# Hybrid attention block: 16 differences of x on VectorE instead of GpSimd, and another order of the weight sums in the token units

## The chip, the cores and the metric

The kernel runs on one core of a Trainium2 chip. The metric is the device time of one execution in microseconds (us). A core has five engines with a queue of instructions each: TensorE (PE in the profile: matmuls; PEld is its loading of weights), VectorE (DVE), ScalarE (ACT), GpSimd (POOL) and SyncE (SP), which here issues nearly all DMAs. Each queue is worked off in order; an instruction waits for the semaphores of what it needs, and everything behind it on its engine waits with it.

## The reference

One decoder block on x of 1024 tokens by 1024 channels, in float32. All projections of the first half come from the same normalised input:

```python
xn = rmsnorm(x, norm1_g[l])
qa, ka, va, qr, kr, vr, gr, gate_a, gate_b = [xn @ wl[:, bounds[i]:bounds[i + 1]] for i in range(len(IN_SPLITS))]
...
y = jax.nn.sigmoid(gate_a) * (o_a @ w_proj_a[l]) + jax.nn.sigmoid(gate_b) * (o_r @ w_proj_b[l])
x = x + y @ w_out[l]
xn2 = rmsnorm(x, norm2_g[l])
x = x + jnp.square(jax.nn.relu(xn2 @ w_up[l])) @ w_down[l]
```

`qa`, `ka`, `va` are the 12 heads of the dilated attention, the others belong to the retention and the gates. The change touches only how `xn`, and the weights of `qa`, `ka` and `va`, are made ready for the products.

## The kernel before

**Products in three matmuls.** Each float32 operand is split in a high part (ScalarE, L365, `xh` or `wh`) and a low part (VectorE, L368, `xl` or `wl`), and each product is three matmuls: high by high, high by low, low by high (L268). A split thus needs ScalarE first and then VectorE.

**Seven products for eight.** Most projections use a Strassen-Winograd scheme: a product of 2 by 2 blocks takes seven block products, N1 to N7, on sums and differences of the blocks. The operands N1, N2 and N3 are blocks of x as they are; N5, N7, N6 and N4 are made of differences and sums. The same holds on the side of the weights, where a token unit has the blocks x11, x12, x21, x22, y12 and y22 (names of the code; "x" there is a weight block, too).

**The values' stage** (start to about 74 us). The eight tiles of 128 tokens are taken in the order 0, 4, 1, 5, 2, 6, 3, 7; steps below are numbered 0 to 7 in this order, and so are the tiles. For each tile: load, sum of squares on ScalarE (L610), scale and offset on VectorE (L381), power -1/2 on GpSimd (L382, 128x1), norm on VectorE in two halves (L613, `xn`), transposes on PE (L545, `tr`) in two groups q = 0 and 1, split of the transposes (L365, L368), and a copy `x` of them (L554). Meanwhile PE runs one step for each tile: 24 matmuls that give the first four heads' values, copied out by VectorE (L638, `c`). Behind every second tile, `differences` makes the four operands N5, N7, N6 and N4 of that pair: on GpSimd one subtraction or addition of 128x512 each (L566), then a split of the result.

**The token units** (behind it). Four units `u` of 1024 columns (queries and keys of head pairs, and the other heads' values). Each runs N1, N2, N6, N5, N3, N7, N4, and for each name four groups `t` of 12 matmuls. Their results go in turn to two pools of PSUM banks, `mm` and `ms`, three banks each; VectorE adds them up (L716 for N2, L719 to L732 for the rest). A result that belongs to queries or keys is squared by ScalarE into another bank of `ms` (L690), reduced by VectorE (L691), scaled by GpSimd (L382, L694), and four groups later transposed by PE (L661).

**The weights** are handled by the class `Weights`. `add_tokens` writes down, for each unit, in which order blocks are loaded and in which place of SBUF (0 to 5; a place is free for the next load when its block is in `used`), and a list of steps: each step does the sums of its operand (L121) and its split, into one of six pairs of buffers. A pair is free when PE is through with the unit in it. `p` is 0 or 1: each block has two halves of 512 rows.

**What sets the order.** PE's queue is as written in the program. On the other engines a scheduler puts the instructions in order when the program is built, by its own costs; `keep_in_program_order` pins an instruction, so that it isn't moved ahead or behind others that way. A pinned split pins its ScalarE part.

Of the kernel before, what the change touches and what calls it, by code (L numbers as in the profile page):

```python
# [13 lines left out]
OP = mybir.AluOpType  # L14
# [23 lines left out]
class Weights:  # L38
# [58 lines left out]
    def add_tokens(self, tag, srcs):  # L97

        for u, quads in enumerate(srcs):
            r = {}  # L100
            second = [("x21", 0, 4), ("x22", 0, 2), ("x21", 1, 5), ("x22", 1, 3)]
            if u == 0:
                second = [second[i] for i in (0, 2, 1, 3)]
            for name, p, place in (("x11", 0, 0), ("x11", 1, 1), ("x12", 0, 2), ("x12", 1, 3), *second,
                                   ("y12", 0, 2), ("y12", 1, 3), ("y22", 0, 2), ("y22", 1, 3)):
                r[name, p] = len(self.src)
                self.src.append(quads[{"11": 0, "12": 1, "21": 2, "22": 3}[name[1:]]][p])
                self.place.append(place)
            for name, x, need, ends, sums in (
# [4 lines left out]
                for p in range(2):  # L114
                    buf, key = self.cycle[self.turn % self.WB], (tag, u, name, p)
                    self.turn += 1

                    def step(p=p, x=x, ends=ends, sums=sums, buf=buf, key=key, r=r):
                        for y, z in sums:
                            y, z = self.raw[r[y, p]], self.raw[r[z, p]]  # L120
                            self.nc.vector.tensor_tensor(y, y, z, op=OP.add)  # L121
                        h, l = self.buffer(buf)
                        self.split(h, l, self.raw[r[x, p]])
                        self.units[key] = h, l
                        self.used.update(r[e, p] for e in ends)

                    self.steps.append((self.claim(buf, key), r[need, p], step))
# [124 lines left out]
class Pipe:  # L252
# [24 lines left out]
    def step(self, ps, terms, ends=None, first=True):  # L277
        fns = self.due.pop(self.slot, [])
        n, m = len(terms), len(fns)
        place = {}  # L280
        for j, fn in enumerate(fns):
            place.setdefault(min(n - 1, (j + 1) * n // (m + 1)), []).append(fn)

        def after(i):
            for fn in place.get(i, []):
                fn()
            if ends and i in ends:
                ends[i]()

        self.group(ps, terms, after, first)  # L290
        self.slot += 1
# [23 lines left out]
def hybrid_block(ctx: ExitStack, tc: tile.TileContext, a: dict, out: bass.AP):  # L315
    nc = tc.nc
# [47 lines left out]
    def split(dst_h, dst_l, src, pinned=False):  # L364
        hi = nc.scalar.activation(dst_h, src, AF.Copy)  # L365
        if pinned:
            tc.keep_in_program_order(hi)
        nc.vector.tensor_tensor(dst_l, src, dst_h.bitcast(F), op=OP.subtract)  # L368
# [155 lines left out]
    operands = {"N1": XS[0, 0], "N2": XS[1, 0], "N3": XS[1, 1], "N5": ES[0], "N6": ES[1], "N7": ES[2], "N4": ES[3]}  # L524
# [3 lines left out]
    with ExitStack() as ph:  # L528
# [3 lines left out]
        def cut(t):  # L532
            return slice((t % 4) * P, (t % 4 + 1) * P)
# [6 lines left out]
        def put_transposed(xn, n, q):  # L540
            t = TILES[n]
            pt = tr.tile([P, 4, P], F, name="tr")
            for i in range(4):
                k = 4 * q + i
                nc.tensor.transpose(pt[:, i, :], xn[:, k * P:(k + 1) * P], ident)  # L545
            if q == 0 and t >= 4:
                x01[t] = [px.tile([P, 4, P], R, name=f"x01{i}", bufs=1) for i in "hl"]
                split(*x01[t], pt)
                for i in range(2):
                    nc.sync.dma_start(x01_d[i, :, :, cut(t)], x01[t][i].bitcast(F))  # L550
            else:
                split(*(x[:, :, cut(t)] for x in XS[q, t // 4]), pt)
            x = kept[q, t // 4] = px.tile([P, 4, P], F, name=f"x{q}{t // 4}", bufs=1 if t >= 4 else 2)
            nc.scalar.activation(x, pt, AF.Copy)  # L554
            if q == 1 and t >= 4:
                x = dict(kept)
                differences(t, x, (("N5", (0, 0), (0, 1), OP.subtract), ("N7", (0, 1), (1, 1), OP.subtract)))
                pipe.at(1, lambda: differences(t, x, (("N6", (1, 1), (0, 0), OP.add),
                                                      ("N4", (1, 0), (1, 1), OP.subtract))))
# [3 lines left out]
        def differences(t, x, sums):  # L563

            for name, v, u, op in sums:
                nc.gpsimd.tensor_tensor(x[v], x[v], x[u], op=op)  # L566
                split(*(y[:, :, cut(t)] for y in operands[name]), x[v])

        xts[0] = px.tile([P, D], F, name="xt")
        row = px.tile([P, D], F, name="xn")  # L570
# [54 lines left out]
        for n, t in enumerate(TILES):  # L625
# [9 lines left out]
            ends = {2 * i + 1: (lambda i=i: W.free(us[i])) for i in range(4)} if n == NT - 1 else None  # L635
# [61 lines left out]
    for u in range(len(TOKEN)):  # L697
        n1, part = {}, {}
        for name in ("N1", "N2", "N6", "N5", "N3", "N7", "N4"):
            for t in range(4):  # L700
# [8 lines left out]
                ends = {2 * p + 1: (lambda p=p: W.free(("att", u, name, p))) for p in range(2)} if t == 3 else None  # L709
# [322 lines left out]
    with ExitStack() as ph:  # L1032
# [56 lines left out]
        for d in range(KT):  # L1089
            ub, = W.take(1)  # L1090
            for cs in halves():
                pp = project(0, d, cs, ub)
                t = pm2.tile([P, 512], F, name="s0")
# [15 lines left out]
        for n, (d, cs) in enumerate(work):  # L1109
            if n + 1 < len(work):  # L1110
                ahead.append(fetch(n + 1))
            y, sgb, pa = ahead[n]
# [12 lines left out]
    with ExitStack() as ph:  # L1125
# [54 lines left out]
        for nb in range(2):  # L1180
            us = W.take(4)
            ns = halves()[nb]
            for n, t in enumerate([t for b, t in order if b == nb]):
# [10 lines left out]
                ends = {2 * i + 1: (lambda i=i, us=us: W.free(us[i])) for i in range(4)} if n == NT - 1 else None  # L1194
                pipe.step(pm, terms, ends)
                y = xt
# [15 lines left out]
    with ExitStack() as ph:  # L1212
# [47 lines left out]
        sums = {}  # L1260
# [197 lines left out]
```

## Time and profile before

| | before |
|---|---|
| runs (us) | 2234.1, 2227.32, 2232.43 |
| median (us) | 2232.43 |
| profiled execution, its own time (us) | 2233.11 |
| its span (us) | 2231.0 |
| granted clock of TensorE, mean | 0.996 |
| POOL busy (us) | 201.2 |

The span runs from the first to the last instruction of the profiled execution. The views used are: the page, with busy times; the waits, which say for which engine and line an engine sat idle; windows, one row for each stretch with its length, the busy time of each engine with the number of instructions, the granted clock as a share of full speed, the busy share of the DMA engines and GB/s; the timeline, one row for each instruction with start and duration, and in brackets the idle time ahead of it and what ended it; and the view of one tile. Durations of neighbours on one engine overlap a little, so that the pitch from start to start is what counts.

### The profile page before, as it was taken

To read this page: it belongs to the slowest core of one execution; us is meant where nothing else is said; L and a number is where in the kernel's file an instruction comes from. 1 tells how busy PE (TensorE), PEld (TensorE's weight loads), DVE (VectorE), ACT (ScalarE), POOL (GpSimd) and SP (SyncE) were. 2 spreads that over 40 slices of the span, in tenths; PEclk is the share of its full clock that TensorE was granted. 3 is DMA by queue.
4 is the path that set the end of the run, shared out by engine and by line. 5 is a ranking of instruction groups with operands and counts; after the bars stand their busy time and mean duration, and the time that the engine had idled before them with its cause. 6 is when DMAs were issued, how large, how long until landed. Compare 5 with 4: busy or idle time off the path is not lost.

```text
span 2231.0 us, 28539 instructions
## 1 busy us (share of the span) xinstructions
PE 2181.1 (98%) x10064; PEld 1791.4 (80%) x10064; DVE 1433.8 (64%) x2543; ACT 1109.0 (50%) x1936; POOL 201.2 (9%) x184
## 2 busy tenths in 40 slices
PE   8899999999999999999999999999899999999998
PEld 6788788888788887788888788888788888778887
DVE  6766775555555656657767852363878878686863
ACT  6433544477844567745555633122567777532210
POOL 3313543000000000000000000000000000000002
PEclk9999999999999999999999999999999999999999
DMA  6344434444555545364433484554278899976657
GB/s 228 99 132 114 131 101 128 149 141 146 167 157 163 175 143 165 129 203 134 123 107 98 152 282 159 173 170 152 89 223 248 250 252 280 318 276 236 251 220 174
DMA packets 345665, 392.78 MB, mean 176 GB/s; under 512 B 34738, under 2 KB 270898, under 8 KB 345267
## 3 DMA queue, kind: packets, MB, share of 16 engines
q1 hardware_dynamic: 343026, 386.25, 55.4%
q0 software_dynamic: 2496, 4.72, 1.4%
q8 instruction: 79, 1.29, 0.2%
q14 instruction: 64, 0.52, 0.1%
HBM read 252.39 MB, written 138.51 MB: 175 GB/s over the span
## 4 chain that ended last, share of the span: by engine, by line
PE 78%; DVE 7%; DMA 5%; ACT 5%; issue 3%; POOL 2%; SPq 0%; POOLq 0%; ACTq 0%; DVEq 0%
PE mm L268 45%; PE ms L268 28%; DVE wl L368 2%; DMA raw<-in_w_att_q 1%; PE tr L803 1%; PE tr L822 1%; ACT wh L365 1%; PE tr L661 1%; DVE xl L368 1%; POOL x L566 1%; DMA xl<-h_d 1%; PE tr L815 1%; PE ms L945 1%; PE tr L1001 1%; ACT xh L365 1%
## 5 line engine op out<-in xcount | busy, mean ns | idle before, releaser
L368 DVE TENSOR_TENSOR wl<-raw,wh 128x1024 fp32r<-128x1024 f32 (+1 forms) x292 | 332.4, 1144 | 177.6 <-ACT wh L365 175.7
L365 ACT ACTIVATE wh<-raw 128x1024 fp32r<-128x1024 f32 (+1 forms) x292 | 287.2, 987 | 258.8 <-PE ms L268 125.3
L268 PE MATMUL mm<-xh,wh 128*128 128x512 f32 x896 | 346.3, 410 | 1.5 <-ACT wh L365 1.5
L268 PE MATMUL mm<-xl,wh 128*128 128x512 f32 x896 | 329.2, 391 | 1.7 <-DVE xl L368 1.7
L268 PE MATMUL mm<-xh,wl 128*128 128x512 f32 x768 | 301.0, 392 | 0.5 <-DVE wl L368 0.5
L268 PE MATMUL mm<-wh,xh 128*128 128x512 f32 x736 | 296.6, 403 | 0.0
L268 PE MATMUL mm<-wh,xl 128*128 128x512 f32 x736 | 288.3, 392 | 1.4 <-DMA xl<-h_d 1.4
L268 PE MATMUL mm<-wl,xh 128*128 128x512 f32 x736 | 287.4, 391 | 0.0
L268 PE MATMUL ms<-xh,wh 128*128 128x512 f32 x544 | 226.2, 416 | 2.0 <-DVE St L992 1.2
L268 PE MATMUL ms<-xl,wh 128*128 128x512 f32 x544 | 212.8, 391 | 0.7 <-DVE xl L368 0.7
L268 PE MATMUL ms<-xh,wl 128*128 128x512 f32 x544 | 213.2, 392 | 0.0
L268 PEld LDWEIGHTS mm<-xh,wh 128*128 128x128 f32 x896 | 169.1, 189 | 33.7 <-ACT wh L365 1.9
L268 PEld LDWEIGHTS mm<-xl,wh 128*128 128x128 f32 x896 | 169.0, 189 | 31.7 <-DVE xl L368 2.1
L268 PEld LDWEIGHTS mm<-xh,wl 128*128 128x128 f32 x768 | 144.2, 188 | 31.9 <-DVE wl L368 1.0
L268 PEld LDWEIGHTS mm<-wh,xl 128*128 128x128 f32 x736 | 138.3, 188 | 31.7 <-DMA xl<-h_d 1.8
L268 PEld LDWEIGHTS mm<-wl,xh 128*128 128x128 f32 x736 | 138.9, 189 | 25.8
L268 PEld LDWEIGHTS mm<-wh,xh 128*128 128x128 f32 x736 | 138.6, 188 | 26.2 <-ACT ms L1290 0.4
L268 PE MATMUL ms<-wh,xh 128*128 128x512 f32 x336 | 137.9, 410 | 7.6 <-DVE c L716 4.9
L268 PE MATMUL ms<-wh,xl 128*128 128x512 f32 x336 | 134.7, 401 | 2.4 <-DVE xl L368 2.4
L268 PE MATMUL ms<-wl,xh 128*128 128x512 f32 x336 | 134.0, 399 | 1.2 <-DVE ss L381 0.8
L268 PEld LDWEIGHTS ms<-xh,wh 128*128 128x128 f32 x544 | 102.6, 189 | 23.3 <-DVE St L992 1.6
L268 PEld LDWEIGHTS ms<-xh,wl 128*128 128x128 f32 x544 | 102.2, 188 | 21.8
(284 smaller groups left out, 3816.7 us busy)
## 6 DMA issues: line engine op xcount, KB each, us to landing
h_d<-hs SPq DMA_DIRECT2D x112, 512.0 KB, 4.2
xh<-h_d SPq DMA_DIRECT2D x32, 896.0 KB, 5.9
xl<-h_d SPq DMA_DIRECT2D x32, 896.0 KB, 7.2
raw<-in_w_att_q SPq DMA_DIRECT2D x48, 512.0 KB, 4.3
raw<-in_w_up SPq DMA_DIRECT2D x32, 512.0 KB, 3.8
raw<-in_w_down SPq DMA_DIRECT2D x32, 512.0 KB, 5.5
qk_d<-T SPq DMA_DIRECT2D x48, 256.0 KB, 3.5
raw<-in_w_gate_q SPq DMA_DIRECT2D x16, 512.0 KB, 4.1
```

Source lines behind the costliest of these rows:

```text
L268: self.nc.tensor.matmul(ps, x, y, start=start, stop=stop, skip_group_check=not first)
L365: hi = nc.scalar.activation(dst_h, src, AF.Copy)
L368: nc.vector.tensor_tensor(dst_l, src, dst_h.bitcast(F), op=OP.subtract)
L566: nc.gpsimd.tensor_tensor(x[v], x[v], x[u], op=op)
L661: nc.tensor.transpose(pt[:, i, :], c[:, i * P:(i + 1) * P], ident)
L803: nc.tensor.matmul(sp[:, :w], q[:, e * P:(e + 1) * P], k[:, k0 * P:k0 * P + w], start=True, stop=True)
L815: nc.tensor.transpose(tb[:, j * P:(j + 1) * P], st["p"][:, j * P:(j + 1) * P], ident)
L822: nc.tensor.matmul(po[:, :DH], st["t"][:, j * P:(j + 1) * P], v[:, k0 + j, :], start=(j == 0), stop=(j == nk - 1))
L945: nc.tensor.matmul(sp[:, :P], kT[:, f], qT[:, f], start=(f == 0), stop=(f == 1))
L1001: nc.tensor.transpose(pt[:, f, :], it["o"][:, f * P:(f + 1) * P], ident)
```

## The change

In `differences` the 16 operations go from `nc.gpsimd` to `nc.vector`, pinned, and the split behind each is pinned as well.

In the token units the sums are made in another order. Before, N6 is the sum of three (x22 + x21, then x21 + x11, then x11 + x22) in x11's place, and N5 is x22 + x21 in x22's place. Now x21 + x11 is first, then x22 plus that is N6 (in x22's place), and N5 is N6 - x11 (in x11's place), made with N5's own split. y12's sum takes x22's place in the role of x11 and is pinned. So x11 is released with N5's split, and y12 is loaded into x11's places 0 and 1, not x12's and x22's 2 and 3. Each half has four sums, as before.

```diff
-                                   ("y12", 0, 2), ("y12", 1, 3), ("y22", 0, 2), ("y22", 1, 3)):
+                                   ("y12", 0, 0), ("y12", 1, 1), ("y22", 0, 2), ("y22", 1, 3)):
...
-                    ("N6", "x11", "x22", (), (("x22", "x21"), ("x21", "x11"), ("x11", "x22"))),
-                    ("N5", "x22", "x22", ("x22",), ()), ("N3", "y12", "y12", ("x11", "y12"), (("y12", "x11"),)),
+                    ("N6", "x22", "x22", (), (("x21", "x21", "x11", OP.add), ("x22", "x22", "x21", OP.add))),
+                    ("N5", "x11", "x22", ("x11",), (("x11", "x22", "x11", OP.subtract),)),
+                    ("N3", "y12", "y12", ("x22", "y12"), (("y12", "y12", "x22", OP.add),)),
...
-                        for y, z in sums:
-                            y, z = self.raw[r[y, p]], self.raw[r[z, p]]
-                            self.nc.vector.tensor_tensor(y, y, z, op=OP.add)
+                        for *names, op in sums:
+                            x, y, z = (self.raw[r[i, p]] for i in names)
+                            total = self.nc.vector.tensor_tensor(x, y, z, op=op)
+                            if names[0] == "y12":
+                                self.tc.keep_in_program_order(total)
...
-                nc.gpsimd.tensor_tensor(x[v], x[v], x[u], op=op)
-                split(*(y[:, :, cut(t)] for y in operands[name]), x[v])
+                tc.keep_in_program_order(nc.vector.tensor_tensor(x[v], x[v], x[u], op=op))
+                split(*(y[:, :, cut(t)] for y in operands[name]), x[v], pinned=True)
```

The scheduler answers with another order on VectorE and ScalarE; GpSimd loses the 16 operations and keeps the rest, PE's queue is the same. Lines of the new kernel are 3 higher in this part (1 higher for the sums). Three places on VectorE follow.

The values' stage, from the first result's copy (L638, now L641) on: `x_...<-x_...` are the differences of the first pair of tiles, `xl<-x_...` their splits, `xl<-tr` the splits of transposes, `xn` the next tile's norm. Before:

```order
L638 COPY c<-ms 128x512
L381 TENSOR_SCALAR ss<-ss 128x1
L368 TENSOR_TENSOR wl_290<-raw_208,wh_289 128x1024
L368 TENSOR_TENSOR xl<-x_180,xh 128x4x128
L368 TENSOR_TENSOR xl<-x_260,xh 128x4x128
L613 SCALAR_TENSOR_TENSOR xn<-xt,ss,mm 128x512 x2
L368 TENSOR_TENSOR xl<-tr,xh 128x4x128 x2
L368 TENSOR_TENSOR xl<-x_275,xh 128x4x128
L368 TENSOR_TENSOR xl<-x_193,xh 128x4x128
```

and now:

```order
L569 TENSOR_TENSOR x_180<-x_180,x_260 128x512
L641 COPY c<-ms 128x512
L371 TENSOR_TENSOR wl_290<-raw_208,wh_289 128x1024
L371 TENSOR_TENSOR xl<-x_180,xh 128x4x128
L569 TENSOR_TENSOR x_260<-x_260,x_275 128x512
L384 TENSOR_SCALAR ss<-ss 128x1
L371 TENSOR_TENSOR xl<-tr,xh 128x4x128
L616 SCALAR_TENSOR_TENSOR xn<-xt,ss,mm 128x512
L371 TENSOR_TENSOR xl<-x_260,xh 128x4x128
L616 SCALAR_TENSOR_TENSOR xn<-xt,ss,mm 128x512
L371 TENSOR_TENSOR xl<-tr,xh 128x4x128
L569 TENSOR_TENSOR x_275<-x_275,x_180 128x512
```

The first split of transposes now stands ahead of the next tile's norm, the differences stand among the splits, and the sum of a weight block (raw_216, then raw_218: x21 + x11) comes behind this piece, still inside the stage; raw_218's stands ahead of the norm of tile 4.

The first token unit's N2 (results L716, now L719; raw_798 and raw_797 are y12's first half, raw_810 its second). Before:

```order
L716 TENSOR_TENSOR c<-mm,acc 128x512
L121 TENSOR_TENSOR raw_798<-raw_798,raw_208 128x1024
L691 TENSOR_REDUCE ss<-ms 128x4
L381 TENSOR_SCALAR ss<-ss 128x4
L121 TENSOR_TENSOR raw_810<-raw_810,raw_210 128x1024
L716 TENSOR_TENSOR c<-ms,acc 128x512
```

and now, from the second of the four results on:

```order
L719 TENSOR_TENSOR c<-ms,acc 128x512
L694 TENSOR_REDUCE ss<-ms 128x4
L384 TENSOR_SCALAR ss<-ss 128x4
L719 TENSOR_TENSOR c<-mm,acc 128x512
L694 TENSOR_REDUCE ss<-ms 128x4
L384 TENSOR_SCALAR ss<-ss 128x4
L122 TENSOR_TENSOR raw_797<-raw_797,raw_681 128x1024
L719 TENSOR_TENSOR c<-ms,acc 128x512
L371 TENSOR_TENSOR wl_889<-raw_797,wh_888 128x1024
L122 TENSOR_TENSOR raw_810<-raw_810,raw_693 128x1024
```

The sums of y12 have moved from ahead of the second result to behind the third and the fourth. The other units have the same pattern.

The end of the second unit, N4's results (L732, now L735) and the third unit's first sums (raw_1935 is x22's first half). Before:

```order
L732 TENSOR_TENSOR acc<-mm,acc 128x512
L381 TENSOR_SCALAR ss<-ss 128x4
L121 TENSOR_TENSOR raw_1935<-raw_1935,raw_1732 128x1024
L691 TENSOR_REDUCE ss<-ms 128x4
L121 TENSOR_TENSOR raw_1732<-raw_1732,raw_1547 128x1024
L381 TENSOR_SCALAR ss<-ss 128x4
L732 TENSOR_TENSOR acc<-ms,acc 128x512
```

and now:

```order
L735 TENSOR_TENSOR acc<-mm,acc 128x512
L384 TENSOR_SCALAR ss<-ss 128x4
L122 TENSOR_TENSOR raw_1935<-raw_1935,raw_1732 128x1024
L694 TENSOR_REDUCE ss<-ms 128x4
L122 TENSOR_TENSOR raw_1547<-raw_1935,raw_1547 128x1024
L384 TENSOR_SCALAR ss<-ss 128x4
L735 TENSOR_TENSOR acc<-ms,acc 128x512
```

Ahead of N4's second result (`acc<-ms`) stand as many instructions as before; the sum x21 + x11 of this unit is made earlier, in N5 of the unit before.

More of the change, by code (lines that the diff above doesn't have):

```diff
@@ L116, in add_tokens, with step @@
                     self.turn += 1
-                    def step(p=p, x=x, ends=ends, sums=sums, buf=buf, key=key, r=r):
-                        for y, z in sums:
-                            y, z = self.raw[r[y, p]], self.raw[r[z, p]]
-                            self.nc.vector.tensor_tensor(y, y, z, op=OP.add)
+                    def step(p=p, operand=x, ends=ends, sums=sums, buf=buf, key=key, r=r):
+                        for *names, op in sums:
[3 more added lines that the diff above has]
+                                self.tc.keep_in_program_order(total)
                         h, l = self.buffer(buf)
-                        self.split(h, l, self.raw[r[x, p]])
+                        self.split(h, l, self.raw[r[operand, p]])
                         self.units[key] = h, l
```

## The prediction, made before the run

> **What bounds the kernel now.** I read the page first, for its engine shares, then the waits of PE (TensorE) in the first 110 us, then a table of stretches, then the instructions in order of time. The change touches the values' stage (program start to about 74 us) and the token units behind it.
>
> ```profile
> PE 2181.1 (98%) x10064; PEld 1791.4 (80%) x10064; DVE 1433.8 (64%) x2543; ACT 1109.0 (50%) x1936; POOL 201.2 (9%) x184
> ```
>
> PE is the bound, and only 50 us of the span of 2231.0 us is idle on it. A gain can come only from idle PE time and from time in which PE runs slowly. These are PE's longest waits before 110 us behind its start (us in total, times, longest):
>
> ```profile
> PE ms L268 <- DVE c L716: 3.7, 1, 3.7
> PE ms L268 <- DVE xl L368: 2.4, 1, 2.4
> PE ms L268 <- ACT xh L365: 2.2, 1, 2.2
> ```
>
> The first is in a token unit, the other two in the values' stage. The table of stretches shows a step of that stage without a stop, then the rest of the stage (length, busy time of PE, PEld, DVE, ACT, POOL, granted clock, DMA).
>
> ```profile
> 20.70:27.15 6.45, 6.45 (x34) 5.30 (x32) 6.30 (x7) 3.69 (x7) 5.72 (x4) 1.00 1.05 375
> 27.15:74.25 47.10, 41.63 (x186) 32.90 (x184) 30.55 (x48) 25.82 (x45) 19.99 (x18) 0.93 0.40 119
> ```
>
> Step 1 (24 matmuls and two groups of transposes) takes 6.45 us. Five such steps and one without transposes remain.
>
> ```profile
> 30.20 0.73 PE L268 MATMUL ms<-wh,xl 128*128 128x512 f32 x1 [2.44 <-DVE xl L368]
> 30.73 0.63 PE L268 MATMUL ms<-wh,xh 128*128 128x512 f32 x1
> 31.16 0.63 PE L268 MATMUL ms<-wl,xh 128*128 128x512 f32 x1
> ...
> 40.97 0.63 PE L545 MATMUL tr<-ident,xn 128*128 128x128 f32 x4 [0.88 <-DVE xn L613]
> 41.66 0.39 PE L268 MATMUL ms<-wl,x01h 128*128 128x512 f32 x1
> 41.89 0.40 PE L268 MATMUL ms<-wh,x01l 128*128 128x512 f32 x1
> ...
> 76.97 0.39 PE L268 MATMUL ms<-wh,xh 128*128 128x512 f32 x1
> 79.69 0.39 PE L268 MATMUL mm<-wh,xh 128*128 128x512 f32 x1
> ...
> 93.06 0.39 PE L268 MATMUL mm<-wh,xl 128*128 128x512 f32 x1
> 97.19 0.50 PE L268 MATMUL ms<-wh,xh 128*128 128x512 f32 x1 [3.74 <-DVE c L716]
> 102.10 0.39 PE L268 MATMUL mm<-wh,xl 128*128 128x512 f32 x1
> ```
>
> Twelve matmuls of N1 take 79.69 - 76.97 = 2.72 us, a pitch of 0.227; so a step without transposes is 5.44, and N1 began at 76.97 - 2.72 = 74.25. The stretch needs 5 x 6.45 + 5.44 = 37.69 us and took 47.10: **9.41 us lost**. Three stops are 5.5 of it: 2.4 and 2.2 from the waits, and the 0.88 at 40.97. The other 3.9 is the clock: behind the 2.44 stop the matmuls follow at 31.16 - 30.73 = 0.43 us, and the stretch's granted clock is 0.93. Behind the 0.88 stop the pitch is 41.89 - 41.66 = 0.23, full speed. So a stop over 2 us costs about 1.95 us more than itself (3.9 over two stops), and one under 1 us does not.
>
> The Trainium skill, "TensorE: Matmul & The Clock Gate", Part 1, says that the clock falls after an idle window of about 3.4 us. The row at 30.20 speaks against it: 2.44 us was enough here. By the page only the 3.74 us stop would carry a slow stretch, and the sum below would be smaller by 3.9 us; I go by the rows.
>
> The fourth stop is in N2 of the first token unit. From 93.06 to 102.10 lie 15 pitches, 3.41 us; it took 9.04, **5.63 us lost**.
>
> **The change part by part.** First the 16 differences of x. Why PE stopped at 30.20:
>
> ```profile
> 21.28 5.88 POOL L566 TENSOR_TENSOR x<-x,x 128x512 f32<-128x512 f32 x3 [2.97 <-ACT x L554]
> ...
> 21.99 0.69 DVE L638 COPY c<-ms 128x512 f32<-128x512 f32 x1
> 28.14 1.41 DVE L613 SCALAR_TENSOR_TENSOR xn<-xt,ss,mm 128x512 f32<-128x512 f32 x2 [0.44 <-POOL ss L382]
> 29.46 0.69 DVE L368 TENSOR_TENSOR xl<-tr,xh 128x512 fp32r<-128x512 f32 x1
> ```
>
> GpSimd spent 21.28 to 27.16 on three differences while the reciprocal root of the next tile's norm (L382) stood behind them; VectorE waited for it with the norm (L613), and the split PE needed (29.46) stood behind that. The 2.2 stop has the same shape, through ScalarE. With the differences gone, GpSimd does nothing in this stage but the small powers.
>
> What the differences cost on VectorE isn't in the trace. The rows of the tile x bound it (ns min/median/max):
>
> ```profile
> L566 POOL TENSOR_TENSOR x<-x,x x16: 1260/1302/2153, 21.3 to 74.8; 128x512 f32<-128x512 f32 x16
> L368 DVE TENSOR_TENSOR xl<-x,xh x16: 678/690/1780, 24.2 to 78.0; 128x512 fp32r<-128x512 f32 x16
> 31.13 1.28 DVE L368 TENSOR_TENSOR xl<-x,xh 128x512 fp32r<-128x512 f32 x2
> 32.33 0.17 DVE L641 TENSOR_TENSOR gqk<-gqk 128x12 f32<-128x12 f32 x1
> ```
>
> The nearest row is the same form on the same engine: xl<-x, two sources in SBUF, 128x512. Two of them took 32.33 - 31.13, a pitch of 0.60 us. The upper end is GpSimd's own 1.30. I take 0.60: the differences add 16 x 0.60 = 9.6 us to VectorE. Against that, its split of 0.69 went up to 1.78 in the old run beside GpSimd's differences, and this goes too. The Trainium skill, "SBUF — State Buffer", section "Who interferes with whom", says that a VectorE instruction with two SBUF inputs contends with a GpSimd instruction that reads SBUF; the 1.78 agrees. It changes no term of the sum.
>
> Does VectorE keep up? The order is unchanged up to the copy at 21.99. From there to the last split of the stage's operands the new order has 52 instructions of 512 columns (16 differences, 16 xl<-x, 12 splits of transposes, 8 copies) at 0.60, 10 halves of the norm at 29.46 - 28.14 over two = 0.66, six of 1024 columns at about 1.14, and small ones of 0.8 in all: 31.2 + 6.6 + 6.8 + 0.8 = 45.4 us, to 67.4. The last split that a step of this stage needs (tile 7) stands 9.4 us before that end, at 58.0; PE wants it in the middle of step 7, at 27.15 + 32.25 + 2.72 = 62.1. The tightest is tile 6's first split: 53.1, wanted at 27.15 + 4 x 6.45 + 0.46 = 53.4. One place is late: tile 4's norm stands behind a weight sum that has moved up into this stage (raw_218, 1.14), and PE's transposes stop there for about 0.5 us, less than the 0.88 that stood there before. I add 1.0 for waits on ScalarE that the count leaves out. **This part: 9.41 - 1.5 = 7.9 us.** Without the cover, each us by which VectorE is late is a us of PE.
>
> Now the weights' sums. The old order let VectorE stand in front of blocks that were still on their way:
>
> ```profile
> 79.20 5.88 DVE L121 TENSOR_TENSOR raw<-raw,raw 128x1024 f32<-128x1024 f32 x5
> ...
> 95.31 1.23 DVE L121 TENSOR_TENSOR raw<-raw,raw 128x1024 f32<-128x1024 f32 x1 [0.52 <-DMA raw<-in_w_att_q]
> 96.45 0.68 DVE L716 TENSOR_TENSOR c<-ms,acc 128x512 f32<-128x512 f32 x1
> ```
>
> The sum at 95.31 is the second of y12 (for N3, two products later), and waits for its block. It stands ahead of the N2 result (L716) whose PSUM bank PE wanted at 93.3. In the new order the sums of y12 stand behind the third and fourth N2 results, the number of sums is the same (four per block pair), and two of the five at 79.20 have moved up. So this stop goes whole: **5.63 us.** The blocks of y12 land in the places of x11, which are released by N5's split as x22's were, so no load is later. The block x22 is still the last one that N6 needs, but one sum now stands between it and the split, not two.
>
> Later units show the same pattern on a small scale:
>
> ```profile
> 178.03 1.23 DVE L121 TENSOR_TENSOR raw<-raw,raw 128x1024 f32<-128x1024 f32 x1 [1.01 <-DMA raw<-in_w_att_q]
> 179.91 0.50 PE L268 MATMUL ms<-wh,xh 128*128 128x512 f32 x1 [0.82 <-DVE c L716]
> ...
> 235.61 1.22 DVE L121 TENSOR_TENSOR raw<-raw,raw 128x1024 f32<-128x1024 f32 x1 [0.50 <-DMA raw<-in_w_att_q]
> 240.58 0.63 PE L661 MATMUL tr<-ident,acc 128*128 128x128 f32 x4 [1.92 <-POOL ss L382]
> ```
>
> The 0.82 stop is N2's, behind the y12 sum at 178.03 that waits 1.01 for its block, and goes: **0.8 us.** The 1.92 stop at 240.58, in the change from the second unit to the third, I leave in. It hangs on the x22 sum at 235.61, and behind it stand one reduction and one more sum ahead of N4's second result, in the old order as in the new. If it goes too, it brings 1.92 and its slow stretch of 1.95, 3.9 us.
>
> Sum: 7.9 + 5.63 + 0.8 = 14.3 us off the profiled execution's 2233.11 (its span and 2.1 us around it): 2218.8. That execution is 0.7 above the median of the runs, 2232.43; I forecast 2218.
>
> **The rivals.**
> *VectorE becomes the bound.* If a difference costs half-way to GpSimd's 1.30, 0.95, then the ten ahead of tile 6's split put it 3.5 us late instead of 0.3 early, and the twelve ahead of tile 7's cost about 4 us in all; two of the stops may pass 2 us and add 1.95 each. The stage then brings 7.9 - 4 to 7.9 - 8, the whole 2222 to 2226. For it: VectorE has no reserve in steps 2 to 6. Against it: the 0.60 of the same form.
> *The gain is taken back behind the token units* (transfers or a throttled clock that meet PE sooner): 2233. Against it: PE has no idle time at all in the 130 us around the end of the token units, so no transfer is late there.
>
> ```profile
> 360.00:490.00 130.00, 130.00 (x619) 107.69 (x618) 67.22 (x133) 69.80 (x124) 12.09 (x11) 1.00 0.43 136
> ```
>
> *Slower: the y12 sums, now fixed in VectorE's order, stop it in all four units.* If y12's block comes so late that the sum holds the fourth N2 result past the use of its bank, each unit loses what one lost before: 4 x 5.63 = 22.5, against the 14.3 above gained: 8.2 us slower, 2241. That bank is wanted next by N6's fourth group, three groups of 2.72 with transposes (some 3.2 each), 9.6 us, after N2's end.
>
> ```profile
> DMA to landing us min/median/max: 3.5/4.3/7.5
> ```
>
> The load starts behind N5's split, which waits for N1's buffers, about 2.2 us after N1's end (1.1 on ScalarE, 1.1 on VectorE), so it lands 5.7 to 9.7 us after it; N2 itself takes 10.9. It decides only from about 10 us more.
> *The 240.58 stop goes too*: 3.9 less, 2214.9.
>
> **How the numbers follow.** Forecast 0.68; VectorE the bound 0.15; taken back 0.08; slower 0.04; the extra stop gone 0.05. About 0.3% (6.7 us) is what a measurement of this kernel can tell from no change. Faster by more: 0.68 + 0.05 + half of 0.15, less a little for the executions' own spread of 7 us (2227.32 to 2234.1): 0.79. Slower 0.05, within 0.3% 0.16. The range goes from 2211 (the extra stop gone, with the spread) to 2229 (past VectorE the bound).
>
> **What would show it.** Right: no difference on GpSimd; PE's waits for xl, xh and c in N2 gone; N1 starts near 66 us, not 74; N6 starts some 13.5 us earlier than 101.3; a difference on VectorE at a pitch of 0.60. Wrong: transposes that wait for xn in several steps, a granted clock below 1.0 between 30 and 66 us, or a difference near 1 us. If N1 starts near 66 and the time is still 2230 or more, the loss lies behind the token units and the second rival holds.

## The result and the profile after

| | before | changed |
|---|---|---|
| runs, median (us) | 2232.67 (2234.1, 2227.32, 2232.43, 2232.91) | 2216.38 (2217.06, 2216.04, 2215.47, 2216.72) |
| ratio, 95% interval | | 0.9941 [0.9928, 0.9953] |
| profiled execution, its own time (us) | 2233.11 | 2217.06 |
| its span (us) | 2231.0 | 2215.3 |

The kernel became 0.6% faster, by some 16 us; 2218 was forecast. One of the ten executions of the run e5 below ran at a granted clock of 0.753 and took 2712 us; no ratio counts it. The page of the changed kernel, its span and busy times:

```profile
span 2215.3 us, 28536 instructions
PE 2172.5 (98%) x10064; PEld 1786.1 (81%) x10064; DVE 1437.2 (65%) x2559; ACT 1110.2 (50%) x1936; POOL 169.0 (8%) x168
```

GpSimd lost 16 instructions and 32 us, VectorE gained 16. PE has 43 us of idle time left instead of 50; the rest of the gain is busy time of PE, which fell by 8.6 us with the same number of instructions. The stretches of the changed kernel (length, busy time of PE, PEld, DVE, ACT, POOL, granted clock, DMA share and GB/s): step 1, and from there to the start of N1.

```profile
20.70:27.15 6.45, 6.45 (x33) 5.30 (x32) 6.29 (x11) 4.96 (x10) 0.55 (x1) 1.00 1.06 377
27.15:66.13 38.98, 37.85 (x185) 30.85 (x184) 36.72 (x62) 25.39 (x43) 3.48 (x4) 1.00 0.50 148
```

The second took 47.10 us before and had a granted clock of 0.93. It is now 38.98 long at a clock of 1.00; the work without a stop is 37.69. The waits of PE before 110 us, the longest of the changed kernel:

```profile
PE mm L591 <- DMA xn<-in_norm_g: 4.3, 1, 4.3
PE tr L548 <- DVE xn L616: 1.1, 1, 1.1
```

The first is the program's start, as before. `xl`, `xh` and `c` no longer stop PE. The tile x of the changed kernel (ns min/median/max, first and last start), and the first difference in the order of time:

```profile
L569 DVE TENSOR_TENSOR x<-x,x x16: 680/684/687, 22.0 to 68.1; 128x512 f32<-128x512 f32 x16
L371 DVE TENSOR_TENSOR xl<-x,xh x16: 680/684/694, 24.4 to 69.9; 128x512 fp32r<-128x512 f32 x16
22.04 0.68 DVE L569 TENSOR_TENSOR x<-x,x 128x512 f32<-128x512 f32 x1
22.64 0.68 DVE L641 COPY c<-ms 128x512 f32<-128x512 f32 x1
```

A difference costs 22.64 - 22.04 = 0.60 us of VectorE, and its split never takes longer than 0.69 us, where it went up to 1.78 beside GpSimd's differences.

**An account by stretches.** In every kernel of this study PE runs the same matmuls in the same order, so the same matmul can be looked up in each trace (the one that started at 27.15, 74.25, 101.33 and 345.09 us in the first profile of before). The lengths between them, in us, read from the timeline of PE in each kernel's one profiled execution; the kernels are those of the next section:

| kernel | to step 2 | values' stage from step 2 | N1 and N2 | to 345 | rest | span |
|---|---|---|---|---|---|---|
| before | 27.15 | 47.10 | 27.08 | 243.76 | 1885.9 | 2231.0 |
| before, second execution | 27.42 | 45.68 | 28.15 | 241.09 | 1890.4 | 2232.7 |
| before, third execution | 27.70 | 47.30 | 25.72 | 240.97 | 1883.0 | 2224.7 |
| changed | 27.15 | 38.98 | 21.76 | 240.03 | 1887.4 | 2215.3 |
| changed, again | 28.14 | 38.97 | 21.76 | 239.93 | 1884.8 | 2213.6 |
| differences only (e1) | 27.22 | 38.38 | 23.46 | 240.77 | 1887.0 | 2216.8 |
| weights only (e2) | 27.28 | 43.69 | 21.76 | 239.91 | 1882.2 | 2214.8 |
| powers in order on GpSimd (e3) | 28.01 | 42.84 | 27.62 | 243.07 | 1886.5 | 2228.0 |
| differences not pinned (e4) | 27.89 | 38.98 | 21.76 | 240.17 | 1885.4 | 2214.2 |
| y12 not pinned (e5) | 28.15 | 38.98 | 24.00 | 241.56 | 1883.0 | 2215.7 |
| old sums, y12 pinned (e6) | 27.35 | 38.34 | 21.76 | 239.85 | 1883.2 | 2210.5 |
| 16 more on VectorE (e7) | 27.59 | 39.94 | 27.62 | 239.85 | 1884.6 | 2219.6 |
| all sums pinned (e9) | 27.87 | 38.39 | 21.76 | 239.72 | 1888.6 | 2216.3 |
| e9, differences not pinned (e12) | 27.55 | 39.36 | 21.76 | 240.05 | 1883.7 | 2212.4 |

N1 and N2 without a stop are 8 groups of 2.72, that is 21.76: the changed kernel has nothing left to gain there. The column "to step 2" lies ahead of every edit. "Rest" begins inside the fourth token unit, at the end of its N1, so that its first piece is edited; but from 345.09 to the matmul that started at 430.02, behind the last unit, all 14 executions take 84.93 us. These two columns scatter by 1.0 and 8.2 us from one execution to the next, which is why a difference of a few us is read here from the stretch and not from the whole time.

### The profile page after: what moved, and what is told of

It is laid out like the page before. It is cut to its first block, busy times and chain, and to the rows that moved or that the text cites. A ratio compares the mean times of both kernels' runs of the same rounds, so it can differ in the third digit from the quotient of the medians.

```text
span 2215.3 us, 28536 instructions
## 1 busy us (share of the span) xinstructions
PE 2172.5 (98%) x10064; PEld 1786.1 (81%) x10064; DVE 1437.2 (65%) x2559; ACT 1110.2 (50%) x1936; POOL 169.0 (8%) x168
## 3 DMA queue, kind: packets, MB, share of 16 engines
q8 instruction: 79, 1.29, 0.2%
## 4 chain that ended last, share of the span: by engine, by line
PE 86%; DVE 4%; ACT 4%; issue 3%; DMA 3%; POOL 1%; SPq 0%; POOLq 0%; ACTq 0%; DVEq 0%
PE mm L271 48%; PE ms L271 32%; PE tr L806 1%; PE tr L825 1%; PE tr L664 1%; DVE wl L371 1%; DVE xl L371 1%; PE tr L818 1%; DMA xl<-h_d 1%; PE ms L948 1%; PE tr L1004 1%; ACT wh L368 1%; POOL out L1304 0%; ACT L812 0%; DMA h_d<-hs 0%
```

## The experiments

Ratios are to the kernel before on the same chip, with their 95% interval.

**The change once more (e0).** The same kernel.

> The changed kernel again, beside the same runs of the kernel before as the next three, since each part alone brought about 12 us and the whole 16: a time of 2215 to 2218, and a gain of 13 to 17 us. The parts then overlap by 7 to 11 us. If it comes out near 22 us of gain, they add and the first comparison was off.

2216.03 us, ratio 0.9938 [0.9922, 0.9955]. The three stretches behind step 2 repeat within 0.1 us, so the gain belongs to the kernel. The gain of 13.8 us on this chip is inside the expected 13 to 17.

**The differences alone (e1).** The kernel before with only

```
-                nc.gpsimd.tensor_tensor(x[v], x[v], x[u], op=op)
-                split(*(y[:, :, cut(t)] for y in operands[name]), x[v])
+                tc.keep_in_program_order(nc.vector.tensor_tensor(x[v], x[v], x[u], op=op))
+                split(*(y[:, :, cut(t)] for y in operands[name]), x[v], pinned=True)
```

> The differences on VectorE alone, the weight sums as before. If the two parts are independent and add (theory): N1 of the first token unit starts at 66 us as in the change, the stop of PE in N2 (3.7 us and its slow stretch, 5.5 us in all) is still there, and the time is 8 us below the kernel before, about 2224.5. Rival, the parts help each other (the weight sums that move up into the values' stage are what fills it, or the earlier N1 moves the y12 blocks out of the way): the stop in N2 is gone or under 1 us, or N1 starts later than 68.

2217.85 us, ratio 0.9946 [0.9927, 0.9964], so faster than the 2224.5 that were expected if the parts add. The values' stage is 38.38, even 0.6 shorter than with the whole change. The stop in N2 shrank to between the two expectations, although nothing in the token units was edited. PE in the order of time:

```profile
86.20 0.50 PE L268 MATMUL ms<-wh,xh 128*128 128x512 f32 x1 [1.41 <-DVE c L716]
```

The sum of y12's second half still stands ahead of the second N2 result and waits for its block, but it starts 18.7 us behind the start of N1, where it was 21.1 before.

**The weights' sums alone (e2).** The other hunks of the diff without that one.

> The weight sums in the new order alone, the differences still on GpSimd. Theory (the parts add): N1 starts at 74 to 75 us as before, the stops of PE in N2 of the first and the second unit are gone, and the time is 6.6 us below the kernel before, about 2226. Rival (the sum of x21 that moves up into the values' stage meets GpSimd's differences and holds up VectorE): N1 starts at 77 or later, and 3 us or less is left of the gain.

2219.8 us, ratio 0.9953 [0.9936, 0.9969], where 2226 was expected. N1 and N2 take 21.76: the stop of 3.74 us is gone. Beyond the expectation, the values' stage is 3.4 shorter. Its first stop is there, the one of 0.88 isn't, and the third halved:

```profile
30.36 0.50 PE L271 MATMUL ms<-wh,xl 128*128 128x512 f32 x1 [2.47 <-DVE xl L371]
...
58.61 0.50 PE L271 MATMUL ms<-wh,xh 128*128 128x512 f32 x1 [1.02 <-ACT xh L368]
```

With sums moved up into the stage the scheduler orders VectorE's work there otherwise; which instruction's new place does it wasn't followed up. So **the two parts don't add**. Against the mean of the three executions of before, the sum of the three stretches (values' stage, N1 and N2, to 345) is 315.6 us. The differences alone take off 13.0, the weights alone 10.3, both 14.9: 8.4 us of the two overlap.

**Is it the queue or the work on GpSimd? (e3)** The kernel before, its differences on GpSimd still, but they and the powers of the norm pinned in program order:

```
-        nc.gpsimd.tensor_tensor(dst, dst, half[:, :w], op=OP.pow)
+        p = nc.gpsimd.tensor_tensor(dst, dst, half[:, :w], op=OP.pow)
+        if pinned:
+            tc.keep_in_program_order(p)
...
-                nc.gpsimd.tensor_tensor(x[v], x[v], x[u], op=op)
+                tc.keep_in_program_order(nc.gpsimd.tensor_tensor(x[v], x[v], x[u], op=op))
...
-            rsqrt(ss[:, 1:2], ss[:, 0:1], 1.0 / D)
+            rsqrt(ss[:, 1:2], ss[:, 0:1], 1.0 / D, True)
```

> The kernel before, with the differences still on GpSimd, but they and the powers of the norm pinned there in program order, so that the power of the next tile stands ahead of the third difference. If PE stopped because the power stood behind differences in GpSimd's queue (theory): the stop of 2.4 us at 30 us shrinks below 1 us and takes its slow stretch along, N1 starts 3 to 4.5 us earlier, at 70 to 71; the stop at 60 us, which came through ScalarE's wait for a difference, stays. Rival (what cost the time was GpSimd's 1.3 us for a difference and VectorE slowed down beside it, whatever the order): N1 starts within 1 us of 74.3.

2229.09 us, ratio 0.9989 [0.9979, 0.9999]. GpSimd now, in the order of time:

```profile
22.51 3.81 POOL L568 TENSOR_TENSOR x<-x,x 128x512 f32<-128x512 f32 x2 [3.34 <-ACT x L556]
26.28 0.99 POOL L382 TENSOR_TENSOR ss<-ss,half 128x1 f32<-128x1 f32 x1
27.25 2.97 POOL L568 TENSOR_TENSOR x<-x,x 128x512 f32<-128x512 f32 x2
```

The power of this first pair stands behind two differences instead of three, and the first stop fell from 2.44 to 1.06 us, with VectorE's order unchanged up to there. The stage is 42.84, 4.3 shorter than in the first profile of before. Only 1.8 of it is shorter stops (3.67 for 5.47 in all); the rest came with PE's clock, which was 1.00 in this stage for 0.93. The other 3.9 of the changed kernel's 8.1 did not come: three waits of 1.1 to 1.2 us remain here, on splits of ScalarE and VectorE, and a split beside a difference still takes up to 1.78 us. So about half of the stage's loss went with GpSimd's new order. The stop near 60 us was expected to stay; it fell from 2.15 to 1.21, although the power of that pair stands where it stood, and some splits of ScalarE and VectorE have other places here, so not all of the half is shown to be the power's. Of the whole time little is gained, 2.1 us in the three stretches against the mean of before, since the stop in N2 is still there, 3.98 us long.

**Are the pins needed? (e4, e5)** The changed kernel without the pin of the differences and their splits (e4), and without that of y12's sums (e5):

```
-                tc.keep_in_program_order(nc.vector.tensor_tensor(x[v], x[v], x[u], op=op))
-                split(*(y[:, :, cut(t)] for y in operands[name]), x[v], pinned=True)
+                nc.vector.tensor_tensor(x[v], x[v], x[u], op=op)
+                split(*(y[:, :, cut(t)] for y in operands[name]), x[v])
```

> The change, but the 16 differences on VectorE and their splits are not pinned; the scheduler then puts each first difference and its split ahead of the norm of the next tile. If only the engine matters (theory): N1 starts at 66 to 67.5 us and the time is within 2 us of the change, 2216 to 2218. Rival (the pin is what keeps the norm in time): one or more stops of PE over 2 us, N1 at 69 or later, 2220 or more.

2215.03 us, ratio 0.9931 [0.9913, 0.9949]; the values' stage is 38.98 in both. That pin brings no time here.

```
                             total = self.nc.vector.tensor_tensor(x, y, z, op=op)
-                            if names[0] == "y12":
-                                self.tc.keep_in_program_order(total)
```

> The change without the pin on the sums of y12: the scheduler puts them ahead of the second and the third result of N2 again. Theory (the pin is what removes the stop in N2): PE stops there by 1 to 4 us, as with the differences alone (1.4) or before (3.7), and N6 starts that much later; the time is 1.5 to 6 us above the change. Rival (the other order of the sums and the earlier block do it, and the pin is not needed): no stop over 0.5 us in N2, the time within 1 us of the change.

2219.46 us, ratio 0.9954 [0.994, 0.9967]. VectorE in N2 of the first unit without the pin:

```profile
85.79 1.81 DVE L122 TENSOR_TENSOR raw<-raw,raw 128x1024 f32<-128x1024 f32 x1 [1.55 <-DMA raw<-in_w_att_q]
87.52 0.68 DVE L717 TENSOR_TENSOR c<-ms,acc 128x512 f32<-128x512 f32 x1
```

and PE, which wants that result's bank:

```profile
88.26 0.50 PE L269 MATMUL ms<-wh,xh 128*128 128x512 f32 x1 [1.92 <-DVE c L717]
```

The old shape is back: a sum that waits for its block, with an N2 result behind it. N1 and N2 take 2.2 us more and the units to 345 us 1.5. The new order of the sums alone doesn't prevent it. The same place in the changed kernel:

```profile
85.38 0.69 DVE L719 TENSOR_TENSOR c<-mm,acc 128x512 f32<-128x512 f32 x1 [0.40 <-PE mm L271]
86.80 0.69 DVE L694 TENSOR_REDUCE ss<-ms 128x4 f32<-128x512 f32 x1 [0.73 <-ACT ms L693]
87.52 0.17 DVE L384 TENSOR_SCALAR ss<-ss 128x4 f32<-128x4 f32 x1
87.60 1.22 DVE L122 TENSOR_TENSOR raw<-raw,raw 128x1024 f32<-128x1024 f32 x1
88.73 0.68 DVE L719 TENSOR_TENSOR c<-ms,acc 128x512 f32<-128x512 f32 x1
```

Here the sum comes behind the third result and waits for nothing.

**Does the other order of the sums do anything? (e6)** The differences on VectorE, the old order of the sums and places, and y12's two sums pinned (they are the only steps with one sum):

```
                         for y, z in sums:
                             y, z = self.raw[r[y, p]], self.raw[r[z, p]]
-                            self.nc.vector.tensor_tensor(y, y, z, op=OP.add)
+                            total = self.nc.vector.tensor_tensor(y, y, z, op=OP.add)
+                            if len(sums) == 1:
+                                self.tc.keep_in_program_order(total)
```

> The change with the kernel before's sums (N6 takes x11 with three sums, N5 x22, y12 in x22's places) and only the two y12 sums of a unit held in program order on VectorE. Theory (holding the y12 sums is what removes the stop in N2, the other order of sums does nothing of its own): no stop of over 0.5 us in N2 of any unit, all six x sums of the first unit stand behind N1 again, and N6 of the first unit starts within 1 us of the changed kernel's 87.6; whole 2215 to 2219, ratio to the kernel before about 0.994. Rival (the other order of the sums is needed, since three sums for N6 in one piece hold the first N2 results up): a stop of 1.5 to 4 us in N2 of the first unit, N6 starts 2 to 6 us later, whole 2219 to 2223.

2214.22 us, ratio 0.9943 [0.9927, 0.996]. No stop over 0.5 us in any N2; N1 and N2 take 21.76. The theory held: once the differences are on VectorE, only the pin of the weights' part works. It also shows what the other order costs. The longest stop behind step 1 in the values' stage, in this kernel and then in the changed one (PE in the order of time):

```profile
36.52 0.63 PE L547 MATMUL tr<-ident,xn 128*128 128x128 f32 x4 [0.50 <-DVE xn L615]
```

```profile
36.96 0.63 PE L548 MATMUL tr<-ident,xn 128*128 128x128 f32 x4 [1.13 <-DVE xn L616]
```

The sum of x21 and x11, which the new order lets move up into the stage, makes the norm behind it 0.6 us later. In the whole time the two kernels can't be told apart.

**How much room has VectorE? (e7)** The changed kernel with a minimum of each difference with itself behind it, 16 more operations that leave the values as they are:

```
+                tc.keep_in_program_order(nc.vector.tensor_tensor(x[v], x[v], x[v], op=OP.min))
```

> The change with 16 more instructions on VectorE, one behind each difference (a minimum of the result with itself, two SBUF sources, 128x512, 0.60 us): the difference costs 1.2 us. Theory of the prediction (VectorE has no reserve in the values' stage, so each us is a us of PE): N1 starts 6 to 10 us later, at 72 to 76. Rival (VectorE has room, waits on ScalarE and PE take it up): N1 starts at most 3 us later.

2223.82 us, ratio 0.9969 [0.9958, 0.9981], so 7.8 us more than the changed kernel on the same chip (2216.03) for 9.6 us of VectorE. But the stage lost only 1.0 (39.94): of the two expectations, the rival's. The price is paid in N2:

```profile
85.24 0.51 PE L271 MATMUL ms<-wh,xh 128*128 128x512 f32 x1 [3.96 <-ACT acc L717]
```

ScalarE, in the order of time, shows how the lateness went there:

```profile
78.33 0.63 ACT L368 ACTIVATE xh<-x 128x512 fp32r<-128x512 f32 x1 [3.52 <-DVE x L570]
79.53 1.06 ACT L368 ACTIVATE wh<-raw 128x1024 fp32r<-128x1024 f32 x1 [0.56 <-DVE raw L122]
83.16 1.06 ACT L368 ACTIVATE wh<-raw 128x1024 fp32r<-128x1024 f32 x1 [2.57 <-DVE raw L122]
84.13 0.58 ACT L717 ACTIVATE acc<-mm 128x512 f32<-128x512 f32 x1
```

The copy of N1's results stands behind splits of weights, these behind the sums of the next product's weights, and those behind VectorE's longer list. VectorE's reserve thus lasts through the values' stage; PE runs dry at 85.24 - 3.96 = 81.28, some 14 us behind its end.

**All sums pinned (e9, e12).** What is left in the token units is a stop near 225 us. e9 is the changed kernel with every sum pinned; e12 is e9 with the differences not pinned (their splits still are).

```
-                            if names[0] == "y12":
-                                self.tc.keep_in_program_order(total)
+                            self.tc.keep_in_program_order(total)
```

> The change with all sums of the token units pinned, not only y12's: the sums of x21 leave the values' stage, and at the end of each unit the results of N4 stand ahead of the next unit's sums. Theory (what is left are stops behind sums that the scheduler put too early): the stop of 1.1 us at 37 us and the one of 1.8 us at 225 us go, the time is 2 to 4 us below the change. Rival (the sums, now late, hold up N6's weights): PE waits for wh or wl in N6, the time is the same or higher.

> The change with the differences not held in order and all sums of the weights held in order. Theory (neither hold matters once GpSimd is free of the differences and y12 is held): no stop over 1 us between 18 and 110 us; whole 2213 to 2217, so the same as the changed kernel (2216) within what can be measured. Rival (both holds work against waits that the scheduler's own order brings): a stop over 2 us in the values' stage or in N2 of a unit, whole 2219 or more. The stop near 225 us should be 1.3 to 1.9 in either case, since the T buffers and ScalarE's order stay.

e9: 2215.78 us, ratio 0.9937 [0.9919, 0.9956]; e12: 2216.09, 0.9949 [0.9934, 0.9964]. Neither is faster than the changed kernel by what can be measured: the 2 to 4 us expected of e9 did not come, though its stop near 37 us fell to 0.55. e12 has a stop of 1.12 us at 42.42, a little over its expectation. No sum of the weights stands near 225 us on VectorE any more in e9, and the stop is still 1.34 us. On ScalarE the copy of the transposes, ahead of the stopped ones, waited for a store:

```profile
224.75 0.66 ACT L676 ACTIVATE T<-tr 128x256 f32<-128x256 f32 x2 [1.18 <-DMA qk_d<-T]
```

That the two `T` buffers are the next limit there is read from this row only; no kernel with more of them was run, and in the changed kernel the same copy doesn't wait for a store.

**The clock behind a stop (b1, b2).** The prediction's prices hold a slow stretch for each stop over 2 us. The kernel before was profiled twice more, word for word.

> The kernel before, word for word, in another execution, for the clock behind its stops. Theory (a slow stretch behind a stop depends on when the stop falls in a window of the chip that runs on its own, so one and the same stop has it in one execution and not in another): the stops near 30 (2.4 us), 60 (2.2), 97 (3.7), 240 (1.9) and 1606 us (2.8) are there again within 0.3 us, and at least one of the five changes sides: pitch 0.43 where it was 0.23, or the other way round. Rival (the length of the stop decides, above 2 us or so): all five as in the first profile, slow behind the first four.

> The kernel before, word for word, in a third execution, for the same question. Theory: over the three executions at least two of the five stops (30, 60, 97, 240, 1606 us) are seen both with a slow stretch and without. Rival: none is.

The times were 2234.53 and 2226.43 us. The stop in step 2 in the second execution, then in the third (PE in the order of time):

```profile
30.50 0.50 PE L268 MATMUL ms<-wh,xl 128*128 128x512 f32 x1 [2.47 <-DVE xl L368]
30.84 0.40 PE L268 MATMUL ms<-wh,xh 128*128 128x512 f32 x1
31.07 0.39 PE L268 MATMUL ms<-wl,xh 128*128 128x512 f32 x1
```

```profile
30.83 0.50 PE L268 MATMUL ms<-wh,xl 128*128 128x512 f32 x1 [2.52 <-DVE xl L368]
...
31.54 0.63 PE L268 MATMUL ms<-wl,xh 128*128 128x512 f32 x1
31.96 0.63 PE L268 MATMUL ms<-wh,xl 128*128 128x512 f32 x1
...
97.87 0.50 PE L268 MATMUL ms<-wh,xh 128*128 128x512 f32 x1 [3.67 <-DVE c L716]
98.21 0.40 PE L268 MATMUL ms<-wl,xh 128*128 128x512 f32 x1
98.44 0.39 PE L268 MATMUL ms<-wh,xl 128*128 128x512 f32 x1
```

The stop near 30 us has the pitch of 0.23 behind it in the second execution and 0.42 in the third. Even the 3.67 us stop of N2 has full speed behind it in the third. Over the three executions of before:

| stop (us) | first | second | third |
|---|---|---|---|
| near 30, 2.4 to 2.5 | slow | full | slow |
| near 60, 2.1 to 2.2 | slow | slow | slow |
| near 97, 3.7 to 3.8 | slow | slow | full |
| near 240, 1.8 to 1.9 | slow | full | full |
| near 1606, 2.8 | full | slow | slow |

Four of the five changed sides, so the rival fell: the length of a stop doesn't decide by itself. What decides can be read from the granted clock in the same traces. Behind the first 17 us and up to the last matmul it is 1.00 or 0.50, and it is 0.50 for 3.41 us at a time (once for 6.83). The slow stretches of one execution start whole steps of 3.413 us apart: in the first of before at 30.30, 61.02, 98.56 and 241.92 us, that is 9, 11 and 42 steps. Here are two such steps around the 1.92 us stop of the first execution, then three around the 3.67 us stop of the third (the columns as for the stretches):

```profile
238.51:241.92 3.41, 1.49 (x9) 1.24 (x9) 3.38 (x7) 1.85 (x6) 2.77 (x3) 1.00 0.42 147
241.92:245.33 3.41, 3.41 (x9) 2.54 (x9) 3.41 (x5) 1.78 (x3) 3.30 (x2) 0.50 0.00 0
...
92.67:96.08 3.41, 1.53 (x7) 0.94 (x5) 2.08 (x4) 0.20 (x1) 0.40 (x1) 1.00 0.65 162
96.08:99.49 3.41, 1.62 (x7) 1.36 (x8) 2.68 (x4) 0.60 (x1) 1.96 (x2) 1.00 0.70 219
99.49:102.90 3.41, 3.41 (x18) 2.78 (x17) 2.72 (x5) 2.53 (x3) 2.73 (x3) 1.00 0.20 82
```

The short stop lies in one step, in which PE is idle for 3.41 - 1.49 = 1.92 us, and the next step is slow. The long one is cut in two, 1.88 and 1.79 us, and no step is slow. This holds over all 14 traces. Of some 9000 steps at full speed, 22 have 1.92 us or more of idle PE, and each of them is followed by a slow step; of those with 1.88 us or less only four are, with 1.64 to 1.73 us, all between 1597 and 1617 us, and why these are is open. A slow step in which PE has work throughout costs half of 3.41, that is 1.71 us; the rest of the 1.95 is there without a slow step, too: the 3.67 us stop of the third execution cost 7.37 - 3.40 = 3.97 over its 15 pitches. The Trainium skill, "TensorE: Matmul & The Clock Gate", Part 1, says that the window in which the chip judges PE's activity runs freely and doesn't start with the kernel; the table and the steps, which lie elsewhere in each execution, agree with that.

## Why the prediction was right, and where it was not

The median is 2216.38 for 2218 forecast. Against the profiled execution from which the sum was made, 2233.11, the changed one, 2217.06, is 16.05 shorter; the sum was 14.3.

- **The values' stage, 7.9 forecast, 8.12 measured.** The mechanism held by e1 and e3: the norm's power stood behind GpSimd's differences, and a split beside a difference took up to 1.78 us for 0.69. How the loss divides between the two isn't shown beyond e3. 1.29 us are left (38.98 - 37.69) where 1.5 were put. The stop at tile 4's norm was seen and its cause named; it is 1.13 where 0.5 was written, and the 1.0 for waits on ScalarE hardly came.
- **A difference at 0.60 us on VectorE**: 0.60. The nearest row, of the same form on the same engine, was the right one of the two bounds.
- **N2 of the first unit, 5.63 forecast, 5.64 measured** over the same 15 pitches (9.04 us before, 3.40 now; the column of the table ends ahead of the slow stretch's end and shows 5.32). Right in size. I put it down to both the order of sums and the place of y12's; e5 and e6 show that the pin alone does it.
- **The second unit, 0.8 forecast.** The wait of N2 there is gone. The gain along PE grew from 13.44 at the start of N6 to 14.88 at 180.48 us of before, by 1.44. Of this 0.31 is the end of the slow stretch behind the first unit's stop, and the other two executions of before, against the first, gained 0.5 to 0.6 in the same piece without any change. That leaves about 0.9 for the change.
- **The 1.92 stop at 240.58, left in.** It is still there. PE of the changed kernel:

```profile
225.55 0.63 PE L664 MATMUL tr<-ident,acc 128*128 128x128 f32 x4 [1.79 <-POOL ss L385]
225.94 0.48 PE L271 MATMUL mm<-wh,xh 128*128 128x512 f32 x1
226.25 0.39 PE L271 MATMUL mm<-wl,xh 128*128 128x512 f32 x1
```

  Its slow stretch is not: behind it the matmuls run at full speed, and the gain along PE went from 14.88 to 16.61. Two of three executions of before lack that stretch as well, so this 1.7 us, about as much as the 1.75 by which the sum was short, belongs to the execution, not to the change. That the stop hangs on x22's sum was at most a part of the cause: e9 took the sums away from there, and 1.34 us stayed (1.44 when the changed kernel ran again).
- **The step that failed: "a stop over 2 us costs about 1.95 us more than itself".** It was drawn from one execution in which four stops of the token units and the values' stage all had their slow stretch. In the three together 8 of these 12 have one. It is the idle time of PE within one step of 3.41 us that counts, not the length of the stop, so the price of a stop is a chance, and so is the limit of 2 us. Of the sum's 14.3, 5.8 was put down to the slow clock: 3.9 in the values' stage and 5.63 - 3.74 in N2, three stretches, of which the three executions have seven of nine. The sum came out close because it was compared with the same execution; against the third, whose time was 2226.43, the changed kernel is 9.4 us faster.
- **"VectorE has no reserve in steps 2 to 6" was wrong.** In e7 9.6 us more on VectorE cost the stage 1.0. The place that gave way was N2, behind a chain through ScalarE that the count of VectorE's work to 67.4 us didn't hold.
- **The rivals.** VectorE the bound: no, at 0.60 a difference. Gain taken back behind the token units: no; "rest" is 1887.4, within the 1883.0 to 1890.4 of before, and the piece around the end of the units is 84.93 in all. y12's pinned sums as a new stop in N2: no unit has one. The extra stop at 240.58 gone: no, the stop stayed.

## What to carry to other kernels

A tiny operation on which the next step depends, here a 128x1 power, must not share an in-order queue with long work that isn't urgent: look for what stands ahead of it, not for the engine's busy share (GpSimd was busy for 9% of the span). The same holds for a sum that waits for a load ahead of a result whose bank PE wants; here, beside the differences on VectorE, one pin on such sums did all of it, and the reordering around it nothing that could be seen. A stop of PE has two prices: its own length, and 1.71 us of half clock where it leaves PE idle for some 1.9 us of one step of 3.41; a stop made shorter than that saves both. When two edits mend stops along one chain of work, their gains overlap, and the gain of each is what it brings on top of the other.

## What was not expected of the hardware

Whether a stop is followed by slow matmuls (a pitch of 0.43 us for 0.23) differs from execution to execution of one kernel, for stops from 1.8 to 3.8 us, since the steps of 3.41 us lie elsewhere in each: 1.92 us of idle PE in one step brought half clock, and 3.67 us cut in two (1.88 and 1.79) did not. And some stops far behind the change come and go by themselves. One transpose of the tile `s` in the changed kernel's profile waited

```profile
857.67 0.33 PE L818 MATMUL tr<-ident,s 128*128 128x128 f32 x1 [2.96 <-ACT s L812]
```

2.96 us, and 1.21 when the same kernel ran again; in the kernel before it was 0.16 in the first execution and 2.64 in the second. So one profile of before and one of after can differ by 2 or 3 us at a place that nothing touched.
